# Retention in a hybrid decoder step: all chunk states first, outputs in groups, and PSUM tiles taken together with their target buffers

## The chip, the cores and the metric

The kernel runs on one core of a Trainium2 chip. The metric is the device time of one execution in microseconds; the kernel before is given by the median of three runs.

## The reference

One layer of a decoder whose mixer runs two branches on the same modulated input: A, an RWKV-7 recurrence (16 heads of 64), and B, a retention (4 heads, 128 key and 256 value channels). A prompt of 2048 tokens and 8 sequences of 4 tokens with earlier state go through it. The part that the change touches is the retention of one chunk of 128 tokens, and in branch A the two low-rank maps that give decay and learning rate:

```python
def _retention_chunk(s, q, k, v, log_gamma):
    scores = jnp.einsum('nhid,nhjd->nhij', q, k) * decay[None]
    inner = jnp.einsum('nhij,nhje->nhie', scores, v)
    cross = jnp.einsum('nhid,nhde->nhie', q, s) * jnp.exp(...)
    k_dec = k * jnp.exp(...)
    s_new = s * jnp.exp(L * log_gamma)[None, :, None, None] + jnp.einsum('nhjd,nhje->nhde', k_dec, v)
    return s_new, inner + cross
...
w_log = -jax.nn.softplus(-(w0 + jnp.tanh(wd) @ w_decay_up)) - 0.5
a = jax.nn.sigmoid(a0 + ad @ w_icl_up)
```

## The kernel before

The prompt goes through in 4 segments of 512 tokens. In each, `run` takes 4 heads of branch B, and with each of them two pairs of heads of branch A, in the steps that `ORDER` lists: the gates of B (`ret_gate`, G0 and G1), the inputs and jobs of a pair (P0, P1), the projections of B (R), the retention (S, `ret_math`), the output projection of the head before (O) and the merge of both branches (M0, M1). The last head of the last segment has the order `LAST`, with both pairs first. The decode tokens ride with the second segment's projections and have their own part (`decode`) beside the third's.

Projections are products of weights (`ww`, split in a high and a low half) with the split input (`uh`, `ul`), 24 products of 512 columns for a block of 128 output channels, in PSUM tiles of pool `pp`. A job is 256 tokens of a pair of heads: low-rank maps, decay, the tiles `AR` and `BK`, the products W, a triangular inverse in five levels of half-precision products (`ZX`, `HH`, with the block tiles `bdM`, `bdZ`, `bdH`), then a chain over four chunks of 64 tokens (`ch<-UV,W`, `ch<-tn,Z`, `ch<-UV,BT`, with the outputs in `yy`). The output projection multiplies the merged branches (`mh`, `ml`) with `ww`, at the very end with `wo`, whose tiles take the buffers of `uh` and `ul`.

PSUM has 8 banks: 3 in `pp`, 3 in `sm`, one in `ch` and one in `yy`. All products of the retention, the low-rank maps and the inverse use `sm`. In SBUF the pool `t2` has 6 tiles of 256 columns; the first stage of a job (lines 1205 to 1246) and the loads of low-rank weights take theirs from it.

No instruction is issued where it is written. Each call is recorded by `Plan.add` (line 435) with what it reads and writes, and `schedule` (line 559) then sets one order for all engines: at each step the engine that can start soonest takes, from its operations whose inputs are there, the one that was written first (`choose`, line 693, weighs for PE a change of the array's shape against that). A tile takes a buffer when its first operation is placed, and gives it back after its last; an operation whose tile finds none waits (`misfit`). A tile's first operation is normally the one that writes it, so a PSUM tile is taken by the product that fills it, whether or not the SBUF tile into which it will be read has a buffer. Inside a `bundle()` products follow each other with nothing between them. PSUM tiles count as one piece: a read waits for all products written into the tile before it.

In `ret_math` (line 1694) of before, each chunk computes its output from the scores and the running state `sret`, then its state product `pst` in a bank of its own, then the DVE update of `sret`; the next chunk's output waits for that. Two chunks share an output bank.

Of the kernel before, what the change touches and what calls it, by code (L numbers as in the profile page):

```python
# [14 lines left out]
AF = mybir.ActivationFunctionType  # L15
# [4 lines left out]
MUL, ADD, SUB, MAX = ALU.mult, ALU.add, ALU.subtract, ALU.max  # L20
# [4 lines left out]
JT = 256  # L25
# [381 lines left out]
class Plan:  # L407
# [4 lines left out]
    def __init__(self, tc, ctx):  # L412
        self.tc, self.nc, self.ctx = tc, tc.nc, ctx
        self.ops, self.pools = [], []
        self.tensor, self.vector, self.scalar, self.gpsimd, self.sync = (Eng(self, n) for n in
                                                                        ("PE", "DVE", "ACT", "POOL", "SP"))
        self.prio_off = 0
        self.hold = self.queue = None
        self.open = None

    @contextmanager
    def bundle(self):
# [12 lines left out]
    def add(self, eng, method, a, kw):  # L435
        outs, ins = [], []
        for k, x in list(enumerate(a)) + list(kw.items()):
            if not isinstance(x, View):
                continue
            if (k == 0 and "out" not in kw) or k in _OUTS:  # L440
                outs.append(x)
            else:
                ins.append(x)
        op = Op()
        op.after = []
        op.bundle = ()
        op.eng, op.succ, op.npred, op.ready, op.new, op.tiles = eng, [], 0, 0.0, [], []
        op.num = len(self.ops)
        op.prio = op.num + self.prio_off
        op.sig, op.occ, op.lat = self.cost(eng, method, a, kw, outs, ins)  # L450
        preds = {}
        for x in ins:
            b = x.box()
            for q, c in x.t.writes:
                if _meet(b, c):
                    preds[id(q)] = q
        for x in outs:
            b = x.box()
            for lst in (x.t.writes, x.t.reads):
                for q, c in lst:  # L460
                    if _meet(b, c):
                        preds[id(q)] = q
        for x in outs:
            b = x.box()
            t = x.t
            t.writes = [e for e in t.writes if not _covers(b, e[1])]
            t.reads = [e for e in t.reads if not _covers(b, e[1])]
            t.writes.append((op, b))
        for x in ins:
            x.t.reads.append((op, x.box()))  # L470
        for t in {id(x.t): x.t for x in outs + ins}.values():
            t.nops += 1
            t.last = op
            op.tiles.append(t)
            if t.first is None:
                t.first = op
                op.new.append(t)
                t.tag.order.append(t)
            elif id(t.first) not in preds:
                t.first.after.append(op)  # L480
                op.npred += 1
        if self.hold is not None:
            preds[id(self.hold)] = self.hold
        if eng == "SP" and self.queue is not None:
            if self.queue:
                self.queue[-1].after.append(op)
                op.npred += 1
            self.queue.append(op)
        for q in preds.values():
            if q is not op:  # L490
                q.succ.append(op)
                op.npred += 1
        if self.open is not None and eng == "PE":
            if self.open:
                head = self.open[0]
                for q in preds.values():
                    if q not in self.open and head not in q.succ:
                        q.succ.append(head)
                        head.npred += 1
                head.after.append(op)  # L500
                op.npred += 1
                for t in op.new:
                    t.first = head
                    head.new.append(t)
                op.new = []
            self.open.append(op)
        real = getattr(getattr(self.nc, {"PE": "tensor", "DVE": "vector", "ACT": "scalar", "POOL": "gpsimd",
                                         "SP": "sync"}[eng]), method)
        res = lambda x: x.real() if isinstance(x, View) else x
        op.fn = lambda: real(*[res(x) for x in a], **{k: res(x) for k, x in kw.items()})  # L510
        self.ops.append(op)
        return op
# [295 lines left out]
class Mixer:  # L808
# [396 lines left out]
    def job(self, s, p, j, r, k, v, kn, g, lw):  # L1205
        V, A, G, T = self.V, self.A, self.G, self.T
        cs = slice(j * JT, (j + 1) * JT)
        c3 = lambda a: a.rearrange("p (c t) -> p c t", c=C)
        r3, k3, v2, kn3 = c3(r[:, cs]), k[:, cs], v[:, cs], c3(kn[:, cs])
        ps = self.ps()  # L1210
        self.lora_up(ps[:, 0:JT], lw, 0, cs)
        if j == 0:
            self.lwop = self.pl.ops[-1]
        th = self.t2()
        self.act(th, ps[:, 0:JT], AF.Tanh, bias=self.hw0[:, p:p + 1], scale=0.5)
        sg = self.t2((128, C, 65))
        G.tensor_scalar(out=sg[:, :, 1:65], in0=c3(th), scalar1=1.0, scalar2=1.0, op0=ADD, op1=MUL)
        G.memset(sg[:, :, 0:1], 0.0)
        ps = self.ps()
        self.lora_up(ps[:, 0:JT], lw, 1, cs)  # L1220
        ta = self.t2()
        self.act(ta, ps[:, 0:JT], AF.Tanh, bias=self.ha0[:, p:p + 1], scale=0.5)
        cu = self.t2((128, C, 65))
        V.tensor_tensor_scan(out=cu.rearrange("p c t -> p (c t)"), data0=self.cc("scan"),
                             data1=sg.rearrange("p c t -> p (c t)"), initial=0.0, op0=MUL, op1=ADD)
# [23 lines left out]
        ps = self.ps()  # L1249
# [4 lines left out]
        UV = self.jb.tile([128, C, 2, 64], F32, tag="UV", name="UV", bufs=JB["UV"])  # L1254
        ps = self.ps()
        pv = ps[:, 0:JT].rearrange("p (q t) -> p q t", q=2)
        for q in range(2):
            T.transpose(out=pv[:, q], in_=v2[:, q * 128:(q + 1) * 128], identity=self.ident)
        for e in range(2):
# [48 lines left out]
        ps = self.ps()  # L1308
# [385 lines left out]
    def ret_math(self, s, h):  # L1694
        V, A, G, T = self.V, self.A, self.G, self.T
        q, k, vt = self.qkv
        q4 = q.rearrange("p (c t) -> p c t", t=128)
        k4 = k.rearrange("p (c t) -> p c t", t=128)
        ps = self.ps().rearrange("p (c t) -> p c t", t=128)
        for c in range(4):  # L1700
            T.matmul(ps[:, c], lhsT=k4[:, c], rhs=q4[:, c], start=True, stop=True)
        sct = self.t5((128, 4, 128))
        V.scalar_tensor_tensor(out=sct, in0=ps, scalar=self.cc("rcol")[:, h:h + 1],
                               in1=self.cc("rmask").unsqueeze(1).broadcast_to([128, 4, 128]), op0=MUL, op1=MUL)
        ps = self.ps().rearrange("p (c t) -> p c t", t=128)
        for c in range(4):
            T.transpose(out=ps[:, c], in_=k4[:, c], identity=self.ident)
        kd = self.t5((128, 4, 128))
        self.act(kd, ps, AF.Copy, scale=self.cc("kcol")[:, h:h + 1])
        g128 = float(np.exp(128 * _gammas()[h]))  # L1710
        pe = []
        for half in range(2):
            yt = self.t5((128, 2, 256))
            py = self.ps().rearrange("p (c t) -> p c t", t=256)
            for c2 in range(2):
                c = half * 2 + c2
                T.matmul(py[:, c2], lhsT=sct[:, c], rhs=vt[:, c], start=True, stop=False)
                T.matmul(py[:, c2], lhsT=q4[:, c], rhs=self.sret[:, h], start=False, stop=True)
                pst = self.ps()
                T.matmul(pst[:, 0:256], lhsT=kd[:, c], rhs=vt[:, c], start=True, stop=True)  # L1720
                V.scalar_tensor_tensor(out=self.sret[:, h], in0=self.sret[:, h], scalar=g128, in1=pst[:, 0:256],
                                       op0=MUL, op1=ADD)
            st = self.tiny(12)
            mv = self.tiny(4)
            for c2 in range(2):
                V.bn_stats(out=st[:, c2 * 6:c2 * 6 + 6], in_=py[:, c2])
                V.bn_aggr(out=mv[:, c2 * 2:c2 * 2 + 2], in_=st[:, c2 * 6:c2 * 6 + 6])
            rs = self.rstd(mv[:, 1::2], self.cc("epsr")[:, h:h + 1].broadcast_to([128, 2]), 2)
            for c2 in range(2):
                V.tensor_scalar(out=yt[:, c2], in0=py[:, c2], scalar1=mv[:, 2 * c2:2 * c2 + 1],  # L1730
                                scalar2=rs[:, c2:c2 + 1], op0=SUB, op1=MUL)
            pe.append(yt)
        for e in range(2):
            ps = self.ps()
            for c in range(4):
                T.transpose(out=ps[:, c * 128:(c + 1) * 128], in_=pe[c // 2][:, c % 2, e * 128:(e + 1) * 128],
                            identity=self.ident)
            V.scalar_tensor_tensor(out=self.ob[e], in0=ps, scalar=0.25, in1=self.ob[e], op0=MUL, op1=MUL)
# [232 lines left out]
```

## Time and profile before

| | |
|---|---|
| median of 3 runs | 3203.3 us (3198.7 to 3205.12) |
| the profiled execution | 3193.49 us |
| its span, first to last instruction | 3191.7 us |
| instructions | 64507 |
| mean granted TensorE clock | 0.983 |
| PE matmul busy | 3027.7 us |
| PE weight load busy | 2352.9 us |
| DVE busy | 2197.5 us |
| ACT busy | 1450.6 us |
| POOL busy | 1024.8 us |

Busy time is the union of an engine's instructions; matmuls are pipelined, so rows of the timeline overlap, and the distance between two starts says what an instruction took of the engine. The granted clock is a share of 2.4 GHz. In names, `out<-in`, the buffer number is left out; `sm`, `pp`, `ch`, `yy` and `po` are PSUM tiles. All instructions carry the line of the planner, so they are told apart by tile names. fp32 products run as two passes, which the timeline shows as two rows or as x2.

### The profile page before, as it was taken

To read this page: it belongs to the slowest core of one execution; us is meant where nothing else is said; L and a number is where in the kernel's file an instruction comes from. 1 tells how busy PE (TensorE), PEld (TensorE's weight loads), DVE (VectorE), ACT (ScalarE), POOL (GpSimd) and SP (SyncE) were. 2 spreads that over 40 slices of the span, in tenths; PEclk is the share of its full clock that TensorE was granted. 3 is DMA by queue.
4 is the path that set the end of the run, shared out by engine and by line. 5 is a ranking of instruction groups with operands and counts; after the bars stand their busy time and mean duration, and the time that the engine had idled before them with its cause. 6 is when DMAs were issued, how large, how long until landed. Compare 5 with 4: busy or idle time off the path is not lost. (4 is left out here: it accounts for less than half of the span.)

```text
span 3191.7 us, 64507 instructions
## 1 busy us (share of the span) xinstructions
PE 3027.7 (95%) x24700; PEld 2352.9 (74%) x24700; DVE 2197.5 (69%) x6035; ACT 1450.6 (45%) x3740; POOL 1024.8 (32%) x1453
## 2 busy tenths in 40 slices
PE   8999999997998999999999999999999998999996
PEld 5777677766887898988775666677686776667675
DVE  2667677777786746476686886675767687675777
ACT  4455555545535444353521354534444324454552
POOL 4454444533252222221211422222222353323231
PEclk9999999998999999999999999999999999999997
DMA  8554544635344242333545522324243372324321
GB/s 324 188 193 172 179 165 166 212 125 176 102 153 145 97 149 97 122 109 113 160 139 198 202 95 72 133 99 154 101 160 111 120 242 79 133 92 138 114 97 37
DMA packets 132797, 451.89 MB, mean 142 GB/s; under 512 B 30500, under 2 KB 41636, under 8 KB 92680
## 3 DMA queue, kind: packets, MB, share of 16 engines
q0 software_dynamic: 33120, 241.19, 22.0%
q1 hardware_dynamic: 99368, 206.58, 19.1%
q8 instruction: 194, 3.18, 0.4%
q14 instruction: 115, 0.94, 0.1%
HBM read 345.83 MB, written 101.88 MB: 140 GB/s over the span
## 5 line engine op out<-in xcount | busy, mean ns | idle before, releaser
L510 PE MATMUL pp<-uh,ww 128*128 128x512 f32 (+1 forms) x5152 | 1500.0, 368 | 19.7 <-DMA ww<-wc_wf 7.2
L510 PEld LDWEIGHTS pp<-uh,ww 128*128 128x128 f32 x5152 | 880.4, 190 | 133.6 <-issue 7.6
L510 PE MATMUL pp<-ul,ww 128*128 128x512 f32 (+1 forms) x2576 | 886.3, 365 | 0.2
L510 PEld LDWEIGHTS pp<-ul,ww 128*128 128x128 f32 x2576 | 468.0, 190 | 51.6 <-issue 3.4
L510 ACT CAST ZX<-sm 128x512 f16<-128x512 f32 (+1 forms) x384 | 210.8, 549 | 331.0 <-PE sm L510 299.9
L510 POOL DMA_DIRECT2D ww<-wc_wf x190 | 110.6, 582 | 610.1 <-PE pp L510 414.7
L510 POOL TENSOR_TENSOR ww<-fx,ww 128x512 fp32r<-128x512 f32 x178 | 234.1, 1330 | 183.5 <-ACT ww L510 170.8
L510 DVE COPY bdZ<-ZX 64x256 f16<-64x256 f16 x640 | 182.4, 285 | 107.4 <-ACT ZX L510 98.0
L510 ACT ACTIVATE tn<-UV,PL 64x64 f32<-64x64 f32 x512 | 176.6, 345 | 164.9 <-DVE UV L510 153.8
L510 POOL TENSOR_TENSOR tn<-tn,mhalf 128x2 f32<-128x2 f32 (+2 forms) x108 | 100.0, 926 | 444.0 <-DVE tn L510 442.0
L510 DVE COPY bdH<-HH 64x256 f16<-64x256 f16 x768 | 226.8, 295 | 13.0
L510 PE MATMUL pp<-ww,mh 128*128 128x256 f32 x960 | 202.4, 296 | 3.6 <-DVE zt L510 2.2
L510 POOL TENSOR_TENSOR t<-t,t 128x256 f32<-128x256 f32 (+2 forms) x160 | 140.6, 879 | 181.4 <-ACT t L510 172.3
L510 PE MATMUL pp<-ww,uh 128*128 128x256 f32 x1024 | 175.8, 293 | 0.0
L510 PEld LDWEIGHTS pp<-ww,mh 128*128 128x128 f32 x960 | 155.6, 193 | 10.4 <-issue 1.8
L510 ACT ACTIVATE UV<-ch 64x64 f32<-64x64 f32 x256 | 55.5, 217 | 219.3 <-PE yy L510 213.1
L510 DVE TENSOR_TENSOR HH<-sm,lev 128x256 f16<-128x256 f32 x320 | 134.7, 421 | 25.3 <-PE sm L510 17.8
L510 DVE TENSOR_SCALAR UV<-ch 64x64 f32<-64x64 f32 x256 | 58.3, 228 | 135.6 <-ACT UV L510 89.0
L510 POOL TENSOR_TENSOR bdL<-W,B 64x256 f16<-64x256 f32 x128 | 90.6, 708 | 178.1 <-ACT B L510 101.0
L510 PEld LDWEIGHTS pp<-ww,uh 128*128 128x128 f32 x1024 | 140.5, 190 | 2.4 <-issue 0.4
L510 PE MATMUL pp<-ww,ml 128*128 128x256 f32 x480 | 140.5, 293 | 0.0
L510 DVE SCALAR_TENSOR_TENSOR UV<-ch,PL,tn 64x64 f32<-64x64 f32 x384 | 108.2, 282 | 35.2 <-PE ch L510 27.0
(252 smaller groups left out, 5744.9 us busy)
## 6 DMA issues: line engine op xcount, KB each, us to landing
ww<-wc_wf POOLq DMA_DIRECT2D x190, 1024.0 KB, 5.2
wc_wf<-ww SPq DMA_DIRECT2D x65, 1024.0 KB, 5.6
fx<-in_wf SPq DMA_DIRECT2D x140, 256.0 KB, 3.2
ww<-wc_wv POOLq DMA_DIRECT2D x24, 1024.0 KB, 5.1
ww<-wc_wo POOLq DMA_DIRECT2D x16, 1024.0 KB, 5.1
wa<-in_wa SPq DMA_DIRECT2D x16, 512.0 KB, 7.7
wc_wv<-ww SPq DMA_DIRECT2D x8, 1024.0 KB, 5.3
fx<-in_wo SPq DMA_DIRECT2D x32, 256.0 KB, 2.9
```

Of the source, the lines that this page charges most:

```text
L510: op.fn = lambda: real(*[res(x) for x in a], **{k: res(x) for k, x in kw.items()})
```

## The change

1. `ret_math`: the state products of all four chunks come first, two chunks in one bank and one bundle; DVE makes the three states in between in `t2` tiles and the last in `sret`. The outputs follow, both products of two chunks in one bundle. The scores and the transposes of k are bundles too.
2. `Plan` gets `reserve`: tiles named there take their buffer with the next operation. So the PSUM tile of the low-rank maps is taken together with the two `t2` tiles of their tanh, that of the transposes of v with `UV`, and those of the state products with the tiles of the new states.
3. Both low-rank maps of a job stand in one bundle and in two halves of one bank.

```diff
@@ add @@
+        for x in self.reserve:
+            t = x.t
+            t.first = op
+            t.nops += 1
+            t.last = op
+            op.tiles.append(t)
+            t.tag.order.append(t)
+            (op if self.open is None else self.open[0]).new.append(t)
+        self.reserve = ()
@@ job @@
         ps = self.ps()
-        self.lora_up(ps[:, 0:JT], lw, 0, cs)
+        th, ta = self.t2(), self.t2()
+        with self.pl.bundle():
+            self.pl.reserve = (th, ta)
+            for w in range(2):
+                self.lora_up(ps[:, w * JT:(w + 1) * JT], lw, w, cs)
...
-        th = self.t2()
...
-        ps = self.ps()
-        self.lora_up(ps[:, 0:JT], lw, 1, cs)
-        ta = self.t2()
-        self.act(ta, ps[:, 0:JT], AF.Tanh, bias=self.ha0[:, p:p + 1], scale=0.5)
+        self.act(ta, ps[:, JT:2 * JT], AF.Tanh, bias=self.ha0[:, p:p + 1], scale=0.5)
...
         pv = ps[:, 0:JT].rearrange("p (q t) -> p q t", q=2)
+        self.pl.reserve = (UV,)
@@ ret_math @@
+        sr = [self.sret[:, h]]
+        for half in range(2):
+            ps = self.ps().rearrange("p (c t) -> p c t", t=256)
+            sr += [self.t2(), self.t2() if half == 0 else sr[0]]
+            with self.pl.bundle():
+                self.pl.reserve = sr[1:3] if half == 0 else sr[3:4]
+                for c2 in range(2):
+                    T.matmul(ps[:, c2], lhsT=kd[:, half * 2 + c2], rhs=vt[:, half * 2 + c2], start=True, stop=True)
+            for c2 in range(2):
+                i = 2 * half + c2
+                V.scalar_tensor_tensor(out=sr[i + 1], in0=sr[i], scalar=g128, in1=ps[:, c2], op0=MUL, op1=ADD)
         for half in range(2):
             yt = self.t5((128, 2, 256))
             py = self.ps().rearrange("p (c t) -> p c t", t=256)
-            for c2 in range(2):
-                c = half * 2 + c2
-                T.matmul(py[:, c2], lhsT=sct[:, c], rhs=vt[:, c], start=True, stop=False)
-                T.matmul(py[:, c2], lhsT=q4[:, c], rhs=self.sret[:, h], start=False, stop=True)
-                pst = self.ps()
-                T.matmul(pst[:, 0:256], lhsT=kd[:, c], rhs=vt[:, c], start=True, stop=True)
-                V.scalar_tensor_tensor(out=self.sret[:, h], in0=self.sret[:, h], scalar=g128, in1=pst[:, 0:256],
-                                       op0=MUL, op1=ADD)
+            with self.pl.bundle():
+                for c2 in range(2):
+                    c = half * 2 + c2
+                    T.matmul(py[:, c2], lhsT=sct[:, c], rhs=vt[:, c], start=True, stop=False)
+                    T.matmul(py[:, c2], lhsT=q4[:, c], rhs=sr[c], start=False, stop=True)
```

PE at the last head's retention, before: the first two state products (`sm<-vt,t_39195`, that tile is the decayed k) and the second chunk's output product with the state (`sm<-sret`), among the products of a job.

```order
L510 MATMUL sm<-vt,t_39195 128x256
L510 MATMUL ch<-UV,BT 64x64 x2
L510 MATMUL yy<-UV,W 64x64 x2
L510 MATMUL sm<-vt,t_39195 128x256
L510 MATMUL sm<-sret,t_38529 128x256
L510 MATMUL ch<-UV,W 64x64 x2
L510 MATMUL pp<-ww,mh 128x256
```

The same place after: `t_39045` holds the scores, `t_39413` is the state after the first chunk, `t_38829` holds q; the four state products stand ahead of this piece.

```order
L520 MATMUL yy<-UV,AR 64x64 x2
L520 MATMUL sm<-vt,t_39045 128x256
L520 MATMUL sm<-sret,t_38829 128x256
L520 MATMUL sm<-vt,t_39045 128x256
L520 MATMUL sm<-t_39413,t_38829 128x256
L520 MATMUL pp<-uh,ww 128x512 x2
L520 MATMUL pp<-ul,ww 128x512
L520 MATMUL ch<-UV,BT 64x64 x2
```

All output products of two chunks now stand together behind the states, and the projections of the input (`pp<-uh`, `pp<-ul`) still go on around them.

PE near the end of the program, before: the last job's chain over its chunks, with the last two state products and the last output product of the retention between.

```order
L510 MATMUL sm<-vt,t_39195 128x256 x2
L510 MATMUL ch<-tn,Z 64x64 x2
L510 MATMUL yy<-UV,AR 64x64 x2
L510 MATMUL sm<-sret,t_38529 128x256
L510 MATMUL ch<-UV,BT 64x64 x2
L510 MATMUL yy<-UV,W 64x64 x2
L510 MATMUL sm<-cst,t_39762 128x128 x4
L510 MATMUL ch<-UV,W 64x64 x2
```

The last job's chain after:

```order
L520 MATMUL ch<-UV,W 64x64 x2
L520 MATMUL pp<-ww,mh 128x256
L520 MATMUL pp<-ww,ml 128x256
L520 MATMUL pp<-ww,mh 128x256
L520 MATMUL ch<-tn,Z 64x64 x2
L520 MATMUL yy<-UV,AR 64x64 x2
L520 MATMUL pp<-ww,mh 128x256
L520 MATMUL pp<-ww,ml 128x256
L520 MATMUL pp<-ww,mh 128x256 x2
L520 MATMUL ch<-UV,BT 64x64 x2
L520 MATMUL yy<-UV,W 64x64 x2
```

The products of the output projection now stand between the chain's steps; the retention's and its transposes stand ahead of them.

## Rows read from the trace of the kernel before

**Rows 1.** Page, busy time of each engine, its share and its instructions.
```profile
PE 3027.7 (95%) x24700; PEld 2352.9 (74%) x24700; DVE 2197.5 (69%) x6035; ACT 1450.6 (45%) x3740; POOL 1024.8 (32%) x1453
```
**Rows 2.** Windows of 200 us: stretch, length, busy us of PE to POOL (xinstructions), clock, DMA.
```profile
600.00:800.00 200.00, 176.99 (x1524) 139.12 (x1522) 150.60 (x414) 103.65 (x265) 78.61 (x94) 0.95 0.46 160
2600.00:2800.00 200.00, 186.62 (x1516) 139.13 (x1515) 140.64 (x408) 94.12 (x235) 60.43 (x92) 0.97 0.33 113
```
**Rows 3.** Windows at the end of the program, the same columns.
```profile
3060.00:3080.00 20.00, 19.79 (x167) 14.67 (x167) 13.75 (x37) 11.96 (x26) 4.43 (x9) 1.00 0.30 106
3140.00:3160.00 20.00, 14.34 (x108) 9.56 (x110) 11.03 (x32) 5.38 (x17) 1.69 (x3) 0.50 0.08 27
3118.85:3179.70 60.85, 46.78 (x381) 36.63 (x378) 43.09 (x132) 18.12 (x55) 11.56 (x14) 0.69 0.07 23
```
**Rows 4.** Timeline of PE at the end: start us, length us, instruction, xcount, idle before.
```profile
3101.76 0.39 PE L510 MATMUL pp<-uh,ww 128*128 128x512 f32 x1
...
3117.82 1.42 PE L510 MATMUL sm<-AR,BK 64*128 64x128 f32 x16
...
3138.09 0.37 PE L510 MATMUL sm<-ZX,bdM 128*128 128x64 f16 x4 [1.56 <-ACT ZX L510]
...
3158.76 1.01 PE L510 MATMUL pp<-wo,mh 128*128 128x256 f32 x3
...
3179.71 0.28 PE L510 MATMUL pp<-wo,mh 128*128 128x256 f32 x1
```
**Rows 5.** Timeline of PE: starts from which the prices of its work are taken.
```profile
3100.15 0.63 PE L510 MATMUL pp<-uh,ww 128*128 128x512 f32 x2
3100.61 0.40 PE L510 MATMUL pp<-ul,ww 128*128 128x512 f32 x1
...
3107.54 0.40 PE L510 MATMUL pp<-ww,mh 128*128 128x256 f32 x2
3107.77 0.28 PE L510 MATMUL pp<-ww,ml 128*128 128x256 f32 x1
...
3119.17 0.33 PE L510 MATMUL ch<-tn,Z 64*64 64x64 f32 x4
...
3119.55 0.39 PE L510 MATMUL pp<-ww,mh 128*128 128x256 f32 x1
```
**Rows 6.** Timeline of PE: first and last output product with the state, two retentions.
```profile
1271.63 0.70 PE L510 MATMUL sm<-sret,t 128*128 128x256 f32 x2
...
1293.36 0.70 PE L510 MATMUL sm<-sret,t 128*128 128x256 f32 x2
...
3085.02 0.70 PE L510 MATMUL sm<-sret,t 128*128 128x256 f32 x2
...
3148.07 1.22 PE L510 MATMUL sm<-sret,t 128*128 128x256 f32 x2
```
**Rows 7.** Timeline of PE: retention pairs beside each other, and one beside projection work.
```profile
119.02 0.59 PE L510 MATMUL sm<-sret,t 128*128 128x256 f32 x2
119.45 0.59 PE L510 MATMUL sm<-vt,t 128*128 128x256 f32 x2
119.89 0.28 PE L510 MATMUL sm<-ZX,bdM 128*128 128x64 f16 x4
...
1271.97 0.60 PE L510 MATMUL pp<-ul,ww 128*128 128x272 f32 x2
1272.41 0.54 PE L510 MATMUL pp<-uh,ww 128*128 128x272 f32 x3
1272.88 0.34 PE L510 MATMUL ch<-UV,W 128*64 128x64 f32 x4
```
**Rows 8.** Groups by form: instruction, xcount, busy us, mean ns, idle before and its releasers.
```profile
L510 PEld LDWEIGHTS sm<-vt,t 128*128 128x128 f32 x256 | 40.5, 195 | 14.0 <-DVE Z L510 6.1 <-DVE sret L510 2.9 <-PE yy L510 0.6
```
**Rows 9.** Waits: who waited for whom, us in total, times, longest us.
```profile
PE sm L510 <- DVE BK L510: 16.2, 8, 11.1
```
**Rows 10.** Timeline of POOL at the end: one half of a split of output weights.
```profile
3097.56 2.54 POOL L510 TENSOR_TENSOR ww<-fx,ww 128x512 fp32r<-128x512 f32 x2 [2.23 <-ACT ww L510]
```

More of the change, by code (lines that the diff above doesn't have):

```diff
@@ L508, in add @@
                                          "SP": "sync"}[eng]), method)
+        for x in self.reserve:
[6 more added lines that the diff above has]
+            (op if self.open is None else self.open[0]).new.append(t)
+        self.reserve = ()
         res = lambda x: x.real() if isinstance(x, View) else x
@@ L1699, in ret_math @@
         ps = self.ps().rearrange("p (c t) -> p c t", t=128)
-        for c in range(4):
-            T.matmul(ps[:, c], lhsT=k4[:, c], rhs=q4[:, c], start=True, stop=True)
+        with self.pl.bundle():
+            for c in range(4):
+                T.matmul(ps[:, c], lhsT=k4[:, c], rhs=q4[:, c], start=True, stop=True)
         sct = self.t5((128, 4, 128))
@@ L1705, in ret_math @@
         ps = self.ps().rearrange("p (c t) -> p c t", t=128)
-        for c in range(4):
-            T.transpose(out=ps[:, c], in_=k4[:, c], identity=self.ident)
+        with self.pl.bundle():
+            for c in range(4):
+                T.transpose(out=ps[:, c], in_=k4[:, c], identity=self.ident)
         kd = self.t5((128, 4, 128))
@@ L1711, in ret_math @@
         pe = []
+        sr = [self.sret[:, h]]
+        for half in range(2):
+            ps = self.ps().rearrange("p (c t) -> p c t", t=256)
+            sr += [self.t2(), self.t2() if half == 0 else sr[0]]
+            with self.pl.bundle():
+                self.pl.reserve = sr[1:3] if half == 0 else sr[3:4]
[4 more added lines that the diff above has]
+                V.scalar_tensor_tensor(out=sr[i + 1], in0=sr[i], scalar=g128, in1=ps[:, c2], op0=MUL, op1=ADD)
         for half in range(2):
@@ L1714, in ret_math @@
             py = self.ps().rearrange("p (c t) -> p c t", t=256)
-            for c2 in range(2):
-                c = half * 2 + c2
-                T.matmul(py[:, c2], lhsT=sct[:, c], rhs=vt[:, c], start=True, stop=False)
-                T.matmul(py[:, c2], lhsT=q4[:, c], rhs=self.sret[:, h], start=False, stop=True)
-                pst = self.ps()
-                T.matmul(pst[:, 0:256], lhsT=kd[:, c], rhs=vt[:, c], start=True, stop=True)
-                V.scalar_tensor_tensor(out=self.sret[:, h], in0=self.sret[:, h], scalar=g128, in1=pst[:, 0:256],
-                                       op0=MUL, op1=ADD)
+            with self.pl.bundle():
+                for c2 in range(2):
+                    c = half * 2 + c2
+                    T.matmul(py[:, c2], lhsT=sct[:, c], rhs=vt[:, c], start=True, stop=False)
+                    T.matmul(py[:, c2], lhsT=q4[:, c], rhs=sr[c], start=False, stop=True)
             st = self.tiny(12)
```

## The prediction

> **What bounds the kernel now.** I read the page first: TensorE (PE) is busy 95% of the span and DVE 69% [rows 1], so a change pays only where PE waits or where its instructions get cheaper. PE's busy time leaves 3191.7 - 3027.7 = 164 us. The windows say where those lie: most stretches of 200 us lose 4 to 8 us, a few lose more, as 600 to 800 (23 us) and 2600 to 2800 (13 us) [rows 2], and the end is the worst. From 3118.85, where the last job's W products are done, to the last matmul at 3179.71, PE is busy 46.78 of 60.85 us at a mean granted clock of 0.69; in 3140 to 3160 the clock is 0.50, the lower of its two levels (1.2 of 2.4 GHz) [rows 3]. The timeline shows why: the last projection matmul has started at 3101.76, and the last job's chain of small products then runs almost alone, each step waiting for ACT or DVE (1.56 us before one of them); the last output projection comes at 3158.76 [rows 4]. Where projection work lies beside a job, PE has no such gaps (19.79 of 20 us in 3060 to 3080 [rows 3]).
>
> Next, the retention. Its four chunks run as a series (state product, DVE update, output product), and the planner spreads them: first to last output product is 21.7 us at one head (1271.63 to 1293.36) and 63.1 us at the last one (3085.02 to 3148.07) [rows 6]. An output tile with one chunk done holds one of the three sm banks nearly all this time, and the jobs, and the state products that would end it, share the other two.
>
> **The change, part by part.** No instruction is added or removed on PE, DVE, ACT or POOL, by the two orders counted over the whole program; only their places change. The sum is made against the profiled execution's own 3193.5 us.
>
> *The end.* The order of after has the last job's W products much earlier against the projections. Behind them stand, in before, 18 pp<-ww products of 256 columns and no projection of 512; in after, 89 projections of 512 columns and 96 pp<-ww of 256 (the 96 pp<-wo stand behind them in both). This is what the second pair of listings shows: the last job's state chain has pp work between all its steps. Prices: 0.46 us for two of 512 columns (3100.15 to 3100.61), 0.23 for two of 256 (3107.54 to 3107.77) [rows 5]. So 89 x 0.23 + 78 x 0.115 = 29.4 us of matmuls that before does earlier lie beside the last job's chain. Is there room? What before does there is 46.78 x 0.69 = 32.3 us at full clock, of 60.85 [rows 3]: 28.5 us free. The stretch then takes 32.3 + 29.4 = 61.7 us, about as long as now, and the 29.4 us are gone from the program ahead of it: 29.4 - 0.9 = 28.5, less 0.6 us of waits such as a well-filled window keeps (0.2 in 20 us [rows 3]). **Taken: -28.** Bounds: -32 if the moved work also leaves its own waits behind (a tenth of it); -16 if each of some 24 steps of the chain is held 0.5 us by two projections ahead of it and the chain, not PE, ends the program. One cover is thinner there: the tiles for the last output weights take the buffers of uh and ul, which are free only when the last projection is done. Before leaves 57 us between that and the first pp<-wo [rows 4]; after leaves 96 pp<-ww and ten small groups of the chain (0.38 us for a ch group with its yy group, 3119.17 to 3119.55 [rows 5]), 96 x 0.115 + 10 x 0.38 = 15 us. POOL has four differences of 1.27 us (2.54 for two [rows 10]) to make in it, 5.1 us, or 10.2 if the products with the gate wait too. So it stays covered by 5 us; uncovered, it would cost that overlap at most.
>
> *The retention's products in groups.* A pair here is one fp32 product in its two passes. Beside its own kind one takes (119.89 - 119.02)/2 = 0.43 us. The one at 1271.63 lies before projection work: from it to the ch group at 1272.88 are 1.25 us, less five products of 272 columns at 0.23 x 272/512 = 0.12 each: 0.63 us [rows 6, 7]. Part of that is the switch to the ch group's shape, which is paid wherever that group stands; the pair itself lies between 0.43 and 0.63, and I take the middle, 0.53. In before 32 of the 192 pairs are followed by another, in after 128. 96 x 0.10 = **-10 us**, spread over 16 retentions; bounds -19 (0.20 each) and +5, since what the pairs no longer break up others do.
>
> Here a page weighs in. The Trainium skill (TensorE: Matmul & The Clock Gate, "Architectural detail") says that PE's queue can pull weight loads ahead of matmuls in flight. By it the grouped passes would hide their loads and cost 0.115 each, a pair 0.23, and the 128 pairs would save 128 x 0.20 = 26 us more. The row at 119.45 speaks against it: 0.44 for two passes with nothing else between them [rows 7], so I give it little.
>
> *Direct waits.* The weight loads of the vt products waited 14.0 us in all, of which DVE's sret 2.9 [rows 8]. The update is now off that path, since all state products stand ahead of the outputs. **-4**, bounds 0 and -14. DVE's updates stay 64; they write t2 tiles, and the last one of a head sret, so the output DMA of the state at the end waits for an earlier instruction than before.
>
> *What is paid.* Three of the six t2 tiles are held from a head's first state products to its outputs. The t2 tiles also carry the first stage of every job (decay, AR, BK). Behind a job that waits for one stand its ACT and POOL instructions and then its PE work; PE has waited for BK 16.2 us in 8 waits already, 2.0 us each [rows 9]. I find no row with three t2 tiles gone; bounds are nothing and 16 x 2.0 = +32. The listings are near the lower end (with the bank, the t2 tile and the bundle, the state and output products of the last head stand within a few rows), and PE has projections to do meanwhile. **+7**, a fifth of it. The two low-rank maps in one bank delay the first tanh by two products, 0.23 us [rows 5], on ACT, which has the time (45% busy [rows 1]): nothing, or 64 x 0.23 = 15 us if the jobs' chains end last everywhere. The v transpose's UV tile: nothing; it only keeps a bank from being taken too early.
>
> The Trainium skill (PSUM — Partial Sum Buffer, "PSUM bank collisions raise a hardware error") asks to guard by bank, not by address, so the first tanh may not read while the second map is written. That is the 15 us above, as the page has it; no row shows two maps in a bank.
>
> Sum: -28 - 10 - 4 + 7 = -35, so 3193.5 - 35 = 3158.5 for an execution like the profiled one. The three timed runs lie at 3198.7 to 3205.12, their median 9.8 us above it; I add that: **3168 us**.
>
> **The rivals.**
> - *More than the end.* A bank less in the retention's hands also fills the other thin windows: 31 of the 36 us lost in the two of [rows 2]: 3137 us. For it: banks are held in every head. Against it: PE there is busy with decode and stage work, which the change doesn't touch.
> - *Filled and given back.* The chain ends the program (-16), the pairs and waits give their 14, the t2 tiles take 11 and the shared bank 15: -4, 3199 us, no difference. For it: 0.69 of DVE is taken, and every chain step passes it.
> - *Slower: the t2 tiles.* If each of 16 retentions makes the next job wait long enough that PE runs out of projections, at 4 us each (twice the mean wait for BK, a third of the longest, 11.1 [rows 9]), +64 stands in place of +7: -42 + 64 = +22, 3225 us. It decides from (28 + 10 + 4)/16 = 2.6 us a head. Against it: the order of after has job products between the parts of a retention.
> - *The shared bank's guard on the path*: +15, 3183.
> - *The weight loads hidden in groups*: -26, 3142.
> - *The change doesn't do what it says*: the listings show that it does; no chance of its own.
>
> **How the numbers follow.** Forecast 0.64 (3168, own range 3152 to 3185); more than the end 0.13; given back 0.10; slower 0.08; the guard 0.03; hidden loads 0.02. The range takes the forecast, the guard, half of more and half of given back: 3138 to 3199. A difference of 0.2%, 6.4 us, is about what measurement can tell from none here. Faster by more: 0.64 + 0.13 + 0.03 + 0.02 = 0.82; within: 0.10; slower: 0.08.
>
> **What would show it.** The end is right if no window after the last job's W products has a clock near 0.50, and if the last projection of 512 columns starts about 40 us before the end of the program, where it is 90 us now (3191.7 - 3101.76 [rows 4]). The grouping: sm<-vt products start 0.22 us apart in fours, and the retention's first to last output product is a few us at every head. The price of t2: waits of PE for BK, or of POOL and ACT for t, well above 16.2 us in all. The forecast falls if PE's idle time from the last W products on stays near 26 us (14.1 up to the last matmul [rows 3] and 12.0 behind it), or if the stretches ahead of the end lose more than they gain.

## The result and the profile after

| | before | after |
|---|---|---|
| median | 3203.0 us (4 runs, 3198.7 to 3205.1) | 3147.7 us (4 runs, 3141.6 to 3152.6) |
| ratio | | 0.9828 [0.9804, 0.9853] |
| the profiled execution | 3193.49 us | 3152.61 us |

The change makes the kernel 55 us faster (1.7%). 3168 was forecast, with a range of 3138 to 3199: sign and range hold. The time lies outside the forecast's own 3152 to 3185, though, and nearer to the rival at 3137: the gain is 20 us larger than the -35 of the sum. The profiled pair shows 41 us, since before's execution lay 9.5 us below its median and after's 4.9 above.

The page of after, busy time of each engine, its share and its instructions:

```profile
PE 3009.9 (96%) x24700; PEld 2347.2 (74%) x24700; DVE 2174.5 (69%) x6035; ACT 1444.2 (46%) x3740; POOL 1020.0 (32%) x1453
```

Windows of after as in [rows 2, 3] (stretch, length, busy us of PE, PEld, DVE, ACT, POOL, clock, DMA); the last one reaches from the last job's W products to the last matmul:

```profile
600.00:800.00 200.00, 181.58 (x1576) 146.59 (x1572) 148.12 (x428) 104.57 (x271) 75.24 (x93) 0.95 0.46 153
2600.00:2800.00 200.00, 195.15 (x1642) 141.95 (x1642) 137.92 (x429) 97.58 (x260) 58.21 (x91) 1.00 0.36 122
3060.00:3080.00 20.00, 19.05 (x163) 14.19 (x162) 16.10 (x50) 8.96 (x24) 3.22 (x5) 1.00 0.37 116
3100.00:3120.00 20.00, 20.00 (x177) 16.29 (x177) 14.12 (x35) 6.79 (x20) 12.25 (x10) 1.00 0.33 94
3065.15:3136.14 70.99, 68.06 (x572) 53.75 (x571) 54.05 (x145) 23.63 (x66) 26.08 (x24) 1.00 0.20 62
```

The same number of PE instructions is 18 us less busy and the span is 41 us shorter. The thin end of [rows 3], 46.78 us busy of 60.85 at a clock of 0.69, is gone: 68.06 of 70.99 at 1.00, with more work in it. The timeline of PE after (start, length, instruction, xcount, idle before) shows what fills it: the last W products, the last projection, the first and the last output products with `wo`.

```profile
3063.73 1.42 PE L520 MATMUL sm<-AR,BK 64*128 64x128 f32 x16
...
3105.28 0.39 PE L520 MATMUL pp<-uh,ww 128*128 128x512 f32 x1
...
3123.11 0.50 PE L520 MATMUL pp<-wo,mh 128*128 128x256 f32 x2 [0.28 <-ACT mh L520]
...
3135.86 0.28 PE L520 MATMUL pp<-wo,mh 128*128 128x256 f32 x1
```

The last projection now starts 3150.8 - 3105.3 = 45.5 us before the end of the span (89.9 in [rows 4]) and 41.6 us behind the start of the last W products instead of 16 us ahead of it. The first product with `wo` waits 0.28 us, for `mh` and not for weights: the thinner cover (17.8 us from the last projection) holds.

Two pieces of the same timeline, outputs of the last head's retention:

```profile
3076.33 0.59 PE L520 MATMUL sm<-sret,t 128*128 128x256 f32 x2
3076.76 0.59 PE L520 MATMUL sm<-vt,t 128*128 128x256 f32 x2
3077.19 0.59 PE L520 MATMUL sm<-t,t 128*128 128x256 f32 x2
...
3079.43 0.59 PE L520 MATMUL sm<-t,t 128*128 128x256 f32 x2
3079.86 0.59 PE L520 MATMUL sm<-vt,t 128*128 128x256 f32 x2
3080.29 0.59 PE L520 MATMUL sm<-t,t 128*128 128x256 f32 x2
```

The group by form (xcount, busy us, mean ns, idle before and its releasers) that answers to [rows 8]:

```profile
L520 PEld LDWEIGHTS sm<-vt,t 128*128 128x128 f32 x256 | 44.3, 190 | 8.6 <-ACT t L520 1.9 <-DVE sret L520 1.0 <-DVE W L520 0.5
```

The wait that answers to [rows 9] (us, times, longest):

```profile
PE sm L520 <- DVE BK L520: 10.2, 12, 6.7
```

First to last output product with a state: 3076.33 to 3080.29, 4 us (63 in [rows 6]), and over the whole trace 4 to 8 us at 15 of the 16 heads, 15 us at one; pairs follow each other every 0.43 us; weight loads of the vt products wait 8.6 us (14.0), of which for DVE's `sret` 1.0 (2.9); PE waits 10.2 us for BK (16.2).

**Where the time went.** The two programs do the same work in another order, so I compare them at equal work: each PE instruction gets the lower quartile of the distances to the next start that its shape has in before, and the sums, an estimate of the work done, are cut at 600, 1050, 1500 and 2100 of their 2265.7 us. In before the cuts lie at 833, 1448, 2106 and 2920 us; the third stage holds the decode.

| stage, us | before | after | the same order again | ret_only | maps_only | after_sm2 |
|---|---|---|---|---|---|---|
| 0 to 833 | 832.8 | -12.9 | +3.6 | -13.8 | -10.1 | -12.2 |
| to 1448 | 614.7 | -2.4 | -0.3 | -2.1 | -1.0 | +7.1 |
| to 2106, with the decode | 658.3 | +6.9 | +3.5 | +8.8 | +3.4 | +38.0 |
| to 2920 | 814.4 | -11.5 | -0.2 | -1.3 | -3.4 | +1.8 |
| to the end | 271.6 | -21.0 | (-23.1) | -4.0 | -21.5 | +3.8 |

"The same order again" is the kernel maps_last2 of below, whose first 18470 of 20896 products stand as in before: a second execution of one order moves a stage by some 4 us. Before's profiled run was well off in the stage with the decode: 658 us, where the profiles of the other kernels with three sm banks have 657 to 672 (mean clock 0.99 there; 0.98 in after and in the second execution). That may be part of why it lay below its median. So the -41 are mainly -13 in the first segment, -12 ahead of the end and -21 in the end.

### The profile page after: what moved, and what is told of

It is laid out like the page before. It is cut to its first block, busy times and chain, and to the rows that moved or that the text cites. A ratio compares the mean times of both kernels' runs of the same rounds, so it can differ in the third digit from the quotient of the medians.

```text
span 3150.8 us, 64557 instructions
## 1 busy us (share of the span) xinstructions
PE 3009.9 (96%) x24700; PEld 2347.2 (74%) x24700; DVE 2174.5 (69%) x6035; ACT 1444.2 (46%) x3740; POOL 1020.0 (32%) x1453
## 5 line engine op out<-in xcount | busy, mean ns | idle before, releaser
L520 POOL DMA_DIRECT2D ww<-wc_wf x190 | 110.2, 580 | 614.7 <-PE pp L520 450.6
L520 DVE COPY bdH<-HH 64x256 f16<-64x256 f16 x768 | 226.4, 295 | 12.2
L520 POOL TENSOR_TENSOR tn<-tn,mhalf 128x4 f32<-128x4 f32 (+2 forms) x108 | 99.6, 922 | 412.8 <-DVE tn L520 412.7
L520 DVE COPY bdZ<-ZX 64x256 f16<-64x256 f16 x640 | 163.1, 256 | 97.0 <-ACT ZX L520 89.1
L520 PE MATMUL pp<-ww,uh 128*128 128x256 f32 x1024 | 182.3, 294 | 3.6 <-DVE t L520 3.5
L520 DVE SCALAR_TENSOR_TENSOR t<-pp,omu,t 128x512 f32<-128x512 f32 (+1 forms) x125 | 78.6, 639 | 84.6 <-ACT tn L520 43.3
```

## The experiments

All ratios are against before, measured beside it. At 3203 us, 0.001 is 3.2 us. Two theories stood at the start. A: the end is a term of its own, worth the projections that come to lie beside the last job. B: the retention carries it all, because it holds a bank less.

**Which part does it.** Each part alone, then all with the last head's retention left as in before, then of parts 2 and 3 only the tile UV.

```diff
# ret_only: ret_math of after, job of before
# maps_only: job of after, ret_math of before
# not_last
-                        self.ret_math(s, h)
+                        (self.ret_math if not last else self.ret_math_old)(s, h)
# map_uv: before, and in job
+        self.pl.reserve = (UV,)
         for q in range(2):
             T.transpose(out=pv[:, q], in_=v2[:, q * 128:(q + 1) * 128], identity=self.ident)
```

> Only part 1 of the change (states first, groups, with the tiles of the states taken by the state products); the jobs as before. Its order has no projection of 512 columns behind the last W products, as before (89 in after). Theory A, the sum of the prediction with the end as a term of its own: the end's 28 us stay away, -10 for the pairs, -4 for the direct waits, +7 for t2: -7 us, ratio 0.998 (0.990 to 1.005). Theory B, the retention carries the change because it holds a bank less: at least 30 of the 55 us, ratio 0.991 or below, and retention spans of a few us at each head.

> Only parts 2 and 3 (the PSUM tiles of the low-rank maps and of the transposes of v taken with their targets, both maps in one bank); the retention as before. Its order has 92 projections of 512 columns behind the last W products, as after (89). Theory A: -28 us from the end, and nothing or +15 from the shared bank: ratio 0.991 (0.988 to 0.997), and no window with a clock near 0.50 before the final norm. Theory B: no difference beyond 0.3%, since the retention still spreads and holds its bank.

> All of after, but the retention of the very last head as in before. Its order has 92 projections behind the last W products, as after. Theory A: the last head's retention does not matter for the end; only its share of the pairs goes: ratio 0.983, as after (0.981 to 0.986). Theory B: the bank held through the last job's chain puts back most of the end, +20 us or more: ratio 0.989 or above.

> Only the tile UV is taken together with the PSUM tile of the transposes of v; all else as before. Its order has 27 projections of 512 columns behind the last W products and all 96 pp<-ww of 256. Theory A, by the same prices: 27 x 0.23 + 78 x 0.115 = 15.2 us move beside the chain: about -15 us, ratio 0.9953 (0.993 to 0.998), with a clock between that of before (0.69) and 1.00 from the last W products to the last matmul. Theory B (the retention carries it): no difference beyond 0.2%.

Measured: ret_only 0.9941 [0.9922, 0.9960], maps_only 0.9881 [0.9860, 0.9901], not_last 0.9833 [0.9811, 0.9854], map_uv 0.9895 [0.9864, 0.9926]. B falls: the retention gives 19 of 55 us, and at the last head nothing that can be measured (not_last and after differ by 0.0005). A's ranges take in ret_only, maps_only and not_last, but its sizes are too small: ret_only was to give 7 us and gave 19, maps_only 28 and gave 38, and map_uv, outside its range, 15 and gave 34. The clock of map_uv from its last W products to its last matmul is 0.92, between 0.69 and 1.00, as stated. The two halves add up, 19 + 38 = 57.

**The end by itself, the shared bank, the low-rank tiles, the states' tiles.**

```diff
# maps_last2: job of after only where s == self.ns - 1 and h >= 2, else job of before; ret_math of before
# map_bank: part 3 alone, maps_only without
-            self.pl.reserve = (th, ta)
-        self.pl.reserve = (UV,)
# map_low: part 3 and the low-rank tiles, maps_only without
-        self.pl.reserve = (UV,)
# ret_nores: ret_only without
-                self.pl.reserve = sr[1:3] if half == 0 else sr[3:4]
```

> Parts 2 and 3 only for the jobs of the last two heads of the last segment; all other jobs and the retention as before. Its order has the same end as with parts 2 and 3 everywhere: 92 projections and all 96 pp<-ww behind the last W products. Theory A, the end with the length read after (61 us of stretch become 71 with some 32 us more work in it, and 3 us more behind the last matmul): -18 us, ratio 0.9944 (0.992 to 0.9965). Theory D, parts 2 and 3 work through the end alone: -38 us, 0.988. Theory E, the end is worth nothing and the gain lies in the ordinary stretches: within 0.2% of 1.

> Only part 3 (both low-rank maps in one bundle and one bank), no tile taken ahead. Its order has no projection behind the last W products. Guard theory (the rival of the prediction): the first tanh waits for both maps on the path, up to +15 us, ratio 1.000 to 1.005. Theory A: the guard costs nothing (ACT is 45% busy) and 37 groups fewer of the low-rank maps save some 0.1 to 0.2 us each, -4 to -7 us: 0.998 to 0.999. Theory C, held banks: one bank instead of two waits for the t2 tile of its tanh (394 us of such waits in all before), so -10 us or more: 0.997 or below.

> Part 3 and the low-rank maps' bank taken together with the two t2 tiles; UV as before. Its order has no projection of 512 columns but 65 (18 before) pp<-ww of 256 behind the last W products: 47 x 0.115 = 5 us at the end. Theory C (a bank that waits for a t2 tile slows the jobs everywhere): the low-rank maps' banks are held some 125 us in all (394 before), and the ratio is 0.993 or below. Theory A: 5 us at the end and the 4 to 7 us of the groups: 0.996 to 0.9975. If the transposes' UV carries parts 2 and 3 alone: 0.998 or above.

> Part 1 without the tiles of the states being taken ahead: order and bundles of the retention as after, jobs as before. With part 1 whole the ratio was 0.9941. If order and groups carry it: 0.994 (0.992 to 0.996). If the taking ahead carries it (a bank with state products that waits for a t2 tile stands in the way of the jobs): 0.998 or above.

Measured: maps_last2 0.9917 [0.9897, 0.9937], map_bank 0.9997 [0.9980, 1.0014], map_low 0.9990 [0.9975, 1.0006], ret_nores 0.9969 [0.9951, 0.9986]. The end by itself is worth 26.6 us (20 to 33): more than A's 18 and outside its range, and less than D's 38, which the interval excludes. The window of maps_last2 from its last W products to its last matmul is that of after:

```profile
3089.70:3160.44 70.74, 69.34 (x575) 53.57 (x574) 52.49 (x147) 24.06 (x66) 24.85 (x24) 1.00 0.21 69
```

The guard on a shared bank costs nothing that can be measured, and the groups of low-rank maps show no gain either (the interval of map_bank allows 6 us). Theory C in its simple form (any bank that waits for a t2 tile slows the jobs) falls with map_low, and A's 0.996 to 0.9975 is missed there too: 0.998 or above was stated for the case that UV carries parts 2 and 3. Without the states' tiles taken ahead, the retention's gain halves, 10 us instead of 19, though the intervals overlap.

**What the banks do.** For each sm tile I took the time from its first product to the last read out of it, matching products and reads to the program in order on each engine, and added it up by what reads it. In before, one case, the last job's transposes of v in the timeline of PE (start, length, instruction, xcount):

```profile
3042.80 0.44 PE L510 MATMUL sm<-cst,t 128*128 128x128 f32 x2
```

Their copy into UV in the timeline of ACT:

```profile
3088.57 1.08 ACT L510 COPY UV<-sm 64x128 f32<-64x128 f32 x4
```

The transposed v sits in its bank for 46.8 us, until the copy into UV has been made. The last four jobs hold theirs for 30, 43, 47 and 47 us, the last retention's outputs for 45 and 31, nearly end to end from 2959 to 3155: one bank of three is away while the last jobs should get ahead. In after the same job's transposes on PE:

```profile
3056.36 0.42 PE L520 MATMUL sm<-cst,t 128*128 128x128 f32 x2
```

The last of their copies on ACT:

```profile
3057.46 0.53 ACT L520 COPY UV<-sm 64x128 f32<-64x128 f32 x2
```

Here the bank is held 1.6 us. Three tests of that: UV with the retention but the low-rank maps as before; a second way to end the wait, with another order; the retention without its bundles.

```diff
# uv_ret: after, but the low-rank maps of job as in before
# uv_after: before, and the transposes of v written behind the W products
         V.tensor_tensor(out=W[:, h], in0=pw[h], in1=ma, op=MUL)
+            wop = self.pl.ops[-1]
...
+        self.pl.hold = wop
         for q in range(2):
             T.transpose(out=pv[:, q], in_=v2[:, q * 128:(q + 1) * 128], identity=self.ident)
+        self.pl.hold = hold
# ret_nobun: ret_only, each bundle in ret_math replaced
-        with self.pl.bundle():
+        if True:
```

> Part 1 and, of part 2, the tile UV alone; the low-rank maps as before, each in its bank without a tile taken ahead. The order has 41 projections of 512 columns behind the last W products (89 in after). If the low-rank maps' half of parts 2 and 3 carries nothing beyond what it moves at the end: the two gains measured apart add up, -34 - 19 = -53 us, ratio 0.983 (0.981 to 0.986), as after. If the three parts need each other: 0.988 or above.

> The kernel before, with the transposes of v written behind the job's W products and held until the second of them is read out; no tile is taken ahead of its operation and the retention is as before. 59 projections stand behind the last W products. Held-bank theory: in before the bank with the transposed v waits for the tile UV, 1095 us in all 64 jobs (17 us each, from the first transpose to the last copy); whatever ends that wait gives the same gain: some 200 to 300 us of holding left, ratio 0.9895 (0.986 to 0.993). If the gain of taking UV ahead is an accident of the order it makes, this other order need not have it: 0.996 or above. If the transposes, now late, hold up the chain that needs UV: slower, above 1.002.

> Part 1 without its bundles: states first and their tiles taken ahead, but the planner may put other work between the products; jobs as before. With part 1 whole 0.9941. If the pairs beside their own kind carry the gain (10 us by the sum of the prediction): half of it goes, 0.997 (0.9955 to 0.9995). If the bank that an unfinished output held (895 us in all in before, 250 with part 1) carries it: 0.994 (0.992 to 0.9955).

Measured: uv_ret 0.9906 [0.9885, 0.9927], uv_after 0.9931 [0.9909, 0.9953], ret_nobun 0.9968 [0.9953, 0.9984]. The three parts need each other: UV and the retention give 34 and 19 alone but 30 together, and the low-rank tiles, worth 3 alone, give the missing 25 on top of them. The sums of holding go with that (us over the program, estimates good to a few per cent; the last column counts projections behind the last W products); why it is so is argued from them, not shown:

| kernel | ratio | v, until UV | retention outputs | low-rank | all sm | projections |
|---|---|---|---|---|---|---|
| before | 1 | 1095 | 895 | 394 | 5046 | 0 |
| map_bank | 0.9997 | 1078 | 775 | 491 | 4958 | 0 |
| map_low | 0.9990 | 1036 | 845 | 124 | 4641 | 0 |
| ret_nores | 0.9969 | 1062 | 241 | 405 | 4571 | 0 |
| ret_nobun | 0.9968 | 1087 | 633 | 398 | 4841 | 0 |
| ret_only | 0.9941 | 1093 | 250 | 465 | 4631 | 0 |
| uv_after | 0.9931 | 142 | 752 | 701 | 4332 | 59 |
| maps_last2 | 0.9917 | 886 | 877 | 376 | 4815 | 92 |
| uv_ret | 0.9906 | 229 | 294 | 637 | 3958 | 41 |
| map_uv | 0.9895 | 208 | 819 | 633 | 4430 | 27 |
| maps_only | 0.9881 | 234 | 823 | 127 | 3849 | 92 |
| not_last | 0.9833 | 234 | 238 | 122 | 3400 | 92 |
| after | 0.9828 | 232 | 202 | 122 | 3395 | 89 |

A bank that one early comer gives up, the next takes: with UV taken ahead the low-rank maps, whose reader needs a t2 tile, hold 633 us instead of 394. Only where all are cut are both the holding low and the last job far ahead. The sums alone do not order the kernels: map_low holds 4641 us and gains 3, maps_last2 holds 4815 and gains 27, and uv_ret holds less than map_uv and gains no more. What does separate them is the last column: all kernels with 0 there lie at 0.9941 or above, all others at 0.9931 or below. The time in which all three sm banks are held at once also points to UV: 641 us in before, 607 in ret_only, 452 in map_uv, 355 in maps_only, 292 in after.

uv_after was to give 0.9895 and gave 0.9931, outside its range; its low-rank maps hold most, 701 us. Its interval excludes an accident of one order (0.996). But its 22 us are what the projections that it moves to the end are worth by the prices of the prediction (59 x 0.23 + 78 x 0.115 = 22.5): it shows that ending the wait in another way brings the end, not that it brings more. map_uv gives 34 where the same prices give 15, and where its other 19 come from is open.

ret_nobun falls in the range of the groups, but does not separate the two theories: without bundles the outputs hold their banks 633 us, not the 250 of ret_only. And ret_nores, with all groups and 241 us of holding, gives 10 us as well.

**A bank taken away.** after with two sm banks.

```diff
-NPP,NSM = 3,3
+NPP,NSM = 3,2
```

> The kernel after, with two sm banks in place of three and one PSUM bank unused. In before the sm banks were held 5046 us in all, 1.58 of 3 on the mean; in after 3395 us, 1.08. Held-bank theory: half a bank came free and gave 55 us, so a whole bank taken away costs at least that twice, and the last job falls behind the projections again (the order has 0 projections behind the last W products, as before): slower than before, ratio 1.005 to 1.04. If the gain of after lies in the groups and in the end as such, and banks are plentiful at 1.08 of 3: the end's 27 us go, the rest stays, ratio 0.99 to 0.997.

Measured: 1.0087 [1.0062, 1.0113], 28 us slower than before and 84 slower than after. Its window over the stage with the decode:

```profile
1455.00:2140.00 685.00, 640.53 (x4916) 472.90 (x4914) 456.01 (x1278) 256.86 (x665) 161.09 (x260) 0.94 0.41 133
```

The same work in after:

```profile
1447.00:2106.00 659.00, 631.98 (x5030) 466.83 (x5029) 469.35 (x1308) 265.70 (x683) 162.29 (x264) 0.98 0.42 137
```

The bank is worth much, but not everywhere: against after (the table of stages) the loss is 31 us beside the decode, 25 at the end, 13 and 10 in the stages between, and nothing in the first 833 us. So banks explain the end, whose gain goes with the third one; for the first 833 us they do not explain the 13 us that after gains, since after_sm2 has them too with two banks.

## Why the prediction held, and where it was off

- **The end, -28: near in size, in part by luck.** Measured alone, -26.6. Its signs came as stated: no window near 0.50 from the last W products to the last matmul, the last projection 45 us before the end, PE's idle time from there 2.9 + 14.7 = 17.6 us instead of 26.1. But the stretch is 71 us, not 62. 20 products of the inverses, a head sum and three retention pairs net more stand behind the last W products than in before, some 2 us that had moved there too. The rest is the term 46.78 x 0.69 = 32.3 us, the chain's own work at full clock, which was too small: of the 68.06 us busy, 68.06 - 29.4 - 2 = 37 are left for it, and 2.9 us stay idle where 0.6 was taken. The span behind the last matmul is 14.7 us, 3 more. So 13 us are given back where 1.5 was taken, and the moved work alone would bring 31 - 13 = 18. What evens it out lies ahead: from the cut at 2920 to the end of the last W products before takes 199 us, after 165 and maps_last2 163, 34 and 36 us less for some 31 us of moved work.
- **Who moves it: wrong.** The listings of the whole change gave the moved work, but the text put the bank down to the retention (its opening, and "a bank less in the retention's hands" in the rival at 3137) and priced the tile UV at nothing ("it only keeps a bank from being taken too early"). That was the lever: 1095 us of a bank, more than the retention's 895; map_uv and uv_after bring projections to the end, and ret_only leaves it as it was (0 projections, -4.0 us in the last stage). The step that failed is that only one of three holders was looked for; the rows of PE's transposes and ACT's copies, 47 us apart, were in the trace of before.
- **The pairs in groups, -10: not shown.** From the start of each retention product to the next start PE takes 104.7 us in all in before, 84.8 in ret_only, 82.8 in ret_nores and 98.8 in ret_nobun: the groups are worth some 20 us there, twice the term; what other products lose in their place is not in this sum. Of the time, ret_only gains 19 us, and without the bundles 10 (intervals [0.9922, 0.9960] and [0.9953, 0.9984]); but ret_nores, with all groups, gains 10 too. PE's busy time does not settle it: it fell by 10.1 us in ret_only, by 13.4 in maps_only without any of these groups, and rose by 12.0 in ret_nores with all of them.
- **Direct waits, -4: right in size.** 14.0 became 8.6; but DVE's `sret`, the wait that the term was about, gave only 1.9 of these 5.4 us (2.9 became 1.0).
- **The t2 tiles, +7: not paid.** The wait for BK fell to 10.2 us (4.1 in ret_only), and the retention alone is 19 us faster, not slower. The tiles of the states are held only from the first state product to the outputs, some 9 us at the last head.
- **The shared bank: nothing, as taken.** The first tanh waits for both maps, and map_bank at 0.9997 shows no cost of that. The Trainium skill (PSUM — Partial Sum Buffer, "PSUM bank collisions raise a hardware error") asks for this guard, by bank and not by address; no run here leaves it out.
- **Hidden weight loads (3142): the price was wrong.** The time came near it by chance. Pairs in groups start 0.43 us apart (3079.43, 3079.86, 3080.29), 0.216 a pass and not 0.115. But the loads do run beside the products. In before, the loads of the product that starts at 119.45 in [rows 7] stand in the timeline of PE's weight loads as

```profile
119.24 0.41 PEld L510 LDWEIGHTS sm<-vt,t 128*128 128x128 f32 x2
```

  They begin 0.21 us ahead of their product, while the one of 119.02 is still running, and one load takes 195 ns [rows 8]. The Trainium skill (TensorE: Matmul & The Clock Gate, "Architectural detail") lets loads be pulled ahead of matmuls in flight, and the trace agrees, in before as in after; nothing was left to hide. Nor does the load set the 0.216: passes of 256 columns with weights of only 32 columns (`pp<-fx,d`, in the decode), whose load takes 114 ns on the mean, start 0.216 us apart too. The 0.115 was the price of a product in one pass (`pp<-ww`), and the row at 119.45, which the prediction read against hidden loads, speaks against that price alone.
- **More than the end (3137): part of it came.** In the two windows it named PE is busy 4.6 and 8.5 us longer, of the 36 us lost there; the windows hold somewhat other work after, since after runs ahead. Its reason, freed banks that let jobs run ahead, is the right one for the end; the result lies between it and the forecast, 11 us from it and 20 from 3168.
- **The 9.8 us between the profiled run and the median** were rightly added: in the later measurements before's medians are 3198.8 to 3206.5 us, and the profiled 3193.5 lies at the low end of its executions.

What the sum lacked is about 20 us: part 1 gave 19 where 7 was taken, and parts 2 and 3 gave 11 beyond the end. By the table of stages 13 us of the gain lie in the first segment, for which the sum had nothing but its share of the retention's terms. Why that stretch gains with almost any of the orders that contain part 1 or parts 2 and 3 whole is not settled; it was not tried apart. So about half of the 55 us, the end, has a cause that the runs show; the other half is measured by parts, and its cause stays open.

## What to carry to other kernels

In a kernel with a planned order, a PSUM bank is taken when its first product is placed; if the tile into which it is to be read has no buffer, the bank is lost for as long. Add up, from the trace, the time from the first product into each tile to its last read, by reader: holders that are far above the length of their own work are the ones to take together with their target, all of them: here the low-rank maps took up much of what UV alone gave free (394 to 633 us). About half of what that was worth shows at the end, where PE has nothing else left: work that can be done any time should still be there when the last chain runs.

## What the runs showed that was not expected

- One PSUM bank of eight less, in one order that the planner then makes, cost 84 us of 3148, though the sm banks of after are held only 3395 of 3 x 3151 us, 36%. By the profiles most of that came beside the decode (31 us, granted clock 0.94 instead of 0.98) and at the end (25 us).
- The same order run twice differed by up to 3.6 us in a stage of 600 to 800 us, and other orders with three sm banks by -2 to +14 us in the stage with the decode, where the mean clock is 0.95 to 0.99: a difference of 5 us there says nothing of a change.
